# New order tables for the five engines of a hybrid encoder layer

## The chip, the cores and the metric

The kernel runs on one core of a Trainium2 chip. The metric is the device time of one execution in microseconds (us). The engines are called PE (TensorE), DVE (VectorE), ACT (ScalarE), POOL (GpSimd) and SP (SyncE, which here issues all the data transfers). "L1762" is line 1762 of the kernel.

## The reference

One layer of a streaming encoder is computed in fp32 for 1024 prompt frames and 64 frames of a running stream with 512 cached positions. Cut to what matters:

```python
D_MODEL, SEQ, DEC_SEQ, PAST_LEN, D_FF = 1024, 1024, 64, 512, 4096
H_FOX, H_SGU, H_SB = 6, 4, 6                       # heads of 64 columns each

q_f, k_f, v_f, log_f, u_g, v_g, q_s, k_s, v_s = in_proj(x, w_in, b_f)   # one projection
c = cumsum(log_f, axis=1)
# forgetting attention: causal softmax with logit + c_t - c_s
o_f = softmax(where(mask, q_f @ k_f.T / 8 + c_q - c_k, -1e30)) @ v_f
# spatial gating in chunks of 128 positions, w_s lower triangular
o_g = gelu(u_g) * (w_s @ layer_norm(gelu(v_g)) + b_s)
# stick-breaking attention, strictly causal
a = exp(log_sigmoid(z) + sum of log_sigmoid(-z) over the positions between)
o_s = where(mask, a, 0) @ v_s
mix = (rms_norm_per_head(concat(o_f, o_g, o_s)) * g_mix) @ w_out
x = layer_norm(ALPHA * x + mix, ln1_g, ln1_b)
x = layer_norm(ALPHA * x + square(relu(x @ w_up)) @ w_down, ln2_g, ln2_b)
```

The new keys, values and log gates of the attention are outputs too.

## The kernel before

Every fp32 operand of a matmul is split into a high part, a copy rounded by ACT, and a low part, the difference, which a helper at L120 (`lo_sub`) takes on DVE or POOL. A product is then three passes on PE: high by high, high by low, low by high. Weights come from memory as f32 (`raw`, `rwo`, `wr`, `rd`), are copied by ACT (L344, L987, L1238) and subtracted at L120 or L988.

The stages follow each other, with overlaps:

1. Input. Blocks of 128 rows of x (`xr`, loaded at L318) are transposed on PE (`xtp`, L327) into `xT`. The projections `kvfox`, `kvsb`, `sgu`, `sgv` run at L368, and the queries (`qfox`, `qsb`) at L509. The head queries are scaled into `qd` (L517, L518), whose other half is copied across partitions by a small transfer (L128).
2. Attention. For each head and pair of query blocks, scores `S` (L567), then for the forgetting heads a reduction with the gate on DVE (`m`, L539) and an exponential on ACT (`T`, L542); for the stick-breaking heads a scan on DVE (L551) and additions on POOL (L553). The rows are transposed on PE (`pt`, L615), split into `pth` (ACT at L583, DVE at L120) and multiplied by the values (`o`, L625 to L628). Meanwhile the rows of w_out are scaled by g_mix (`rwo` loaded at L980, `swo` at L987) and stored to memory (`wo_dr`, L991).
3. Output projection (`mx`, L257) and the first layer norm.
4. Up-projection by a fast scheme that adds and subtracts blocks of the operands first and needs fewer products: banks `zA` to `zD` (L1300) are combined on DVE into `hh` (L1314 to L1320), squared after a relu (L1332), and summed (L1341 to L1344). Sums and blocks are stored (`h_dr`).
5. Down-projection in the same scheme: banks `A`, `B`, `D` (L1762), `h4a` and `h4b` as split operands (L1464). Bank by bank the results are added into `acc` on DVE (L1727 the first time, with the residual, and L1729 later). `awa` holds one of the accumulators for a time. L1432 makes the sums of the weights.
6. Tail. The last additions give row sums as well (L1772), then follow the negated mean (L1836), the squares on ACT (L1841), the scale on POOL (L1831, L1832), and the normalisation, on ACT and POOL (L1856, L1860, L1864) for some blocks and on DVE (L1872, L1874) for others, and the stores (L1865, L1875).

Loops over heads, blocks and panels write the instructions, but they do not set the order that is run. At the end of the build `set_orders` takes the instructions of each engine's queue and chains them in the order of a table, one per engine, so that each queue runs exactly in that order. An instruction whose inputs or buffers are not ready holds all that stand behind it on its engine. Buffers and banks were assigned before that and are the same whatever the tables say. The tables are text: numbers packed and encoded, unpacked by `unpack`.

Of the kernel before, what the change touches and what calls it, by code (L numbers as in the profile page):

```python
# [78 lines left out]
def _build(nc, tc, a, es):  # L79
# [2046 lines left out]
{OJW)cPA8^wfrvs+zwO{7qDCS^%JuEb>zkOQLg91<KD=sH_e-cSiW8I<SZm}A7juu(Va3!Hn#A4L-_Y6<<&hPT4c-`+1T~f6z<&yN;2=XYFB`-!((uLz
99SkWuPzdCXZoxKIj!q(6kos_3)aX8m>KHY>u`Cck}Xa{{1FFnY;MsK~ViH35-1xmRi@-`Li#Q>#1NPQy05cet%2q%6&#EMyK#<GWPKR`v#V-V}sdFUc
SUwVJ-j9@!GG+S=_6ib}Z>3SS@?G1FzTet8whFvTiKLso(L^^=u-Jw1R(@8GihPX!xfby$jQ3&{$VW^xz7Ki;Vru;NbxCL`4Kao`%HM4Mwy{to=WL_EF
^MD3vLJ9wna764uq2U0K5WxXG#!Z}K^EEzoxj|J-N%kG%xX1<fKBW1K9B_R|TnGK({64L9-n%Pj7WH&?G&+VeW(;+wQHt@m58y^yPUva}JXcjm6^aQXc
rZ!?#SCj6A4QZ6;E!#hI4E|sM|@_(b#<8Ev>D1y>G*842xSD&_??;-MWke8<!?)JgjVV*}B_XVB@y-M?V=^5h1xU#U?u||ja^(|J5Kk}N{h(o{O<=b$E  # L2130
iH8vO8hts`bU#pR{v!V@g_-P!y!I=y<_A(w?;@V#lL2YC!?_;f>1{HD)!tiWr#G;Vk^Jd$)H$_^rSj9^J@Ftu@ujF2!PqYd2F-J3{xF%f80m&AdLFXT{
jq$n!KOB^RdK*WK8M<;ut9mVeTfY{4)z?jfadW)<7p1bGQU0eL|+G&1Qu2WM@iZ|gPvcVr!8?3Z_$#aO__z6J>Yua)t;8O89fv_)n)K)wS`}!<o_K66$
Fxu<&rMerOc5s@!sXAODm=C*TnU07cj@V&>4%kZxpjpXAkTLjZXT_g>SQpAniiL9^tKoBcGY6_G2j|UVQ_*Mq-)fTdjqB)12oDG5Yw7yr<FY4=^{fHo|
76d9%}vl@y%%sEIx7SzpgRymOFY`@zPvB4e$5<Vxa{4A%ZUfI!#cJ1>W8f;|;;%-%+jvdBbf!pgj1db}(rJlcvj>kK5Z#c*<e3%qPBUO8$|m(|0c4SJ2
U>YpT-^f3#qUceqFaQi1LLmm4_Fs62qX|X|{s+{q59nt9l#0xI*H1;&kDkEjE#*@&}6#NzXHBstVKW~1uRy*O3Omb|P(qTQ?DlaZ;LwP*~*|2&$f3_ol
Bl%HbBr2;3*s`LaHcugTZWES<2SyUIGnM#!bJ(vy#Zl|=sT0s7JzLvvVv&rN81+362;0Z1*OA!7EIw>PNi-x7<;zi2t1~5KcW>n_7kRB70%gA+B8Wz<Q
V;RSZi>uE+xYpU&dt(wB61~kb5I+Tx33J&Q~Mo7yvG><d#fVfeNs}p;VCoX-RwuEJQqJ&b3cygqCH-*##JVESx;hZ#=3#}Fv9y@ZcwN}@@{~~pI3N`tE
171vK0b_Cm{ySmLEO$8!dhQJ!tExdYYaEnbyFS(jOep9tRbP)sd(ygclU;mYbQEkzDi?{{51i-PNcmvr-W#nbi}J#0qCY<XLAMt0;Uq8dom^I|`i1E*v
S3ywyWQJ)2+S*f!eDK&@TG@2b4OZzX@4O*F<L+FT<MV6+pH4l!A?(<ZXm0L3Xd&}NWSN1Q6V)_`%8n^$kl(Hl&58k!_ZQ6H-@i-ZXt%tw7!NHK@pT?<#
poCVbYmllAIZd@GyP5|A?g1aUvVzhm!8=Toc4C?72(l=DQ8^Ws}K{Bc8i6VlbG>6HgZ`Ft~e;vk;XUw~6ejbA`7AuQ00#~mlV1=0_OVf={%mNv^e$Jis  # L2140
Fjk^fwH2#v@p>2}SMe0&Vr||Z-NQfMlfKO9oJKhc)zN!3GW#5t;Ay7sXCa#fE#d1`;p`IlF<5@yh{!`Hdr$RQau#Dr9*@%HrX=2CAn}qnfWG?(sQrt_W
G=DFSfraRF6%gTXmHLV<JfL&)>Pd4n?y3sq0HK1&}(tR_|$v6oDN0PBgP|q#K|V=H|;=sFe9k>F@!2KcB$TAT^*lyUvBdo4Zq8b&)GsUlqFUS+T@{srQ
!Evhw}{mzJ{Q0*WW{<=RoI){k_|f7%QETNWV3wyk7zP57?5_MLg@ysHd&<zfktkA-&X5$n6u5a7B3u6uHVA{vU%%%(9h{OttULlo6~QO0pkSS*%Hw+%e
PiGG+t|FlXsLwbIB<|0vJ4K$2;yAv+dDO!G(On+qe7b^zOUTe;m>d?#e*BuwT}RH@YR*Bq&*`5<*YKCoIkhkHz-_)*-isc;ajAu@+h4!J0>M$K8IE!Mx
<&wVd2N`~aALN+a(DvT8f&;R0+&`cHC7CH0CXFjhxS=md2t^NkS_u|**I}hIz(SAUem8t8@(w~lN$3@0Zo5xCg_R5rgCj{;thEP<$%;9Ed#Nx87y976;
$Xoj92_@fkSw~9FSacc<-wyw~TxN1^sc<poIb|YegcQ<hFQ6d@JuHf3yhC<`TAVcghVY}scn%^`yjHFy?K92m%XaQ08`1T)eFB@hBRp+Ru^ai;vkTPEw
<B|%V_m%zX*Hg-uauJgXryIqr@SqXciR!^yEWn~#VoY=>xkT40=f59kk_~uW*vL!;!ueH2O!;V`EXGt5}`9MC)-QC)Jwh8OTE-f9~70!-SrPLTi;6`6y
# [3 lines left out]
2x;Tyvyu}8uaH*yY!ltjsN))U9y9VM%~=kyf;2y0iSK;~l2i1829mSEbd@z9-8oiy`c6;DxaVAV=Fm%}r-`BS2vlCG9DNDfVzuX{clOkdUI$9EKj*rLJ
_?yx>#Zf_zW)rf=J#~qG$uXMq<>B6|JJwLoOZQ+Qh_6}UpWs9>W^JtWk#mI-@8QituUdLV`i(|{ns>=_#`X6ely1J+F)@u!I*udev&iCx}cA<EQRYemi
&x%G*_J7c?!b5oXg9>R;!&6jt{WrPfwV2M)*A%bv*g6s22b0^Glj{RK7I^u8Z{7V7R*0;<npojOQ%KWBbg~eusax4!`|fo0gyk9Ve}d$*<k$dE`L>{*?
q}dLwBuEGpmoBK7uc>HgYP=vS=qo~*`5QhPO(607KLV}F#9N^3roBDR9A>E$G1+39ezPw-6KcFR5u=htt8`fbQIu&s6mbvg}48B6E)rhs(#>qaG|-ooY
`kUe(sW0H4)o~W}U?Q(qPAf)GP{{Q)!W>14IWUeAV`Y*>4r|1
# [51 lines left out]
A5E=@EP@7tH*h|!n`FerKN4s-t7B~!u^olrrTtXVX8xP?G@vd?fQss7?*PNTQm$io_VWp%xepIGR~WU^YEXq8_$00y@1ugtBgkO4OjRl1E<5E^arYaib  # L2207
# [26 lines left out]
```

## Time and profile before

| | us |
|---|---|
| median of 3 runs (lowest to highest) | 1385.33 (1384.52 to 1386.87) |
| the profiled execution | 1386.09 |
| its span, first to last instruction | 1384.4 |
| PE busy | 1317.4 (95%), 8827 matmuls |
| DVE busy | 980.4 (71%) |
| ACT busy | 728.0 (53%) |
| POOL busy | 606.4 (44%) |
| mean granted clock of PE | 0.994 |

An engine counts as busy while it runs an instruction, not while it waits or issues a transfer. A row of the timeline gives start, busy time, engine, line, operation, output and inputs, shapes, and how many alike follow each other; in brackets stands how long the engine was idle before it and what it then waited for. Matmuls overlap in the pipeline, so one that shows 0.4 us can follow another after 0.2 us. Waits of an engine are listed as: who waited for whom, us in total, times, longest.

### The profile page before, as it was taken

The numbers are of one execution on the slowest core, as the hardware profiler recorded it, in microseconds if no ns is written. First come the engines' busy times: TensorE is split into PE (matmuls) and PEld (weight loads), VectorE is DVE, ScalarE is ACT, GpSimd is POOL, SyncE is SP. The second block draws the span as 40 slices with busy tenths as digits, with TensorE's granted clock in tenths as the row PEclk, the third lists the DMA queues.
The fourth block names the chain that finished last, engine by engine and source line by source line (L and its number), as shares of the span: only waits on it lengthen the run. The fifth ranks groups of instructions, "written<-read, shape, count | busy, mean of one in ns | idle before, by whom it ended". The sixth has DMA issues, their size and how long they took to land.

```text
span 1384.4 us, 24306 instructions
## 1 busy us (share of the span) xinstructions
PE 1317.4 (95%) x8827; PEld 1197.6 (87%) x8827; DVE 980.4 (71%) x1795; ACT 728.0 (53%) x1561; POOL 606.4 (44%) x667
## 2 busy tenths in 40 slices
PE   7888899999999999999999999999989999999996
PEld 7888899989998899777799999999977778887874
DVE  4566656566788368779865878777786777767776
ACT  4465646466666466334432323223266676767773
POOL 3221313226666354676512212212176675665556
PEclk9999999999999999999999999999999999999999
DMA  8655414132221346632234444444558344435333
GB/s 254 181 164 169 131 50 127 42 80 67 76 51 42 82 131 219 222 118 84 76 118 152 142 146 142 134 154 142 183 186 289 127 134 167 141 118 172 113 116 121
DMA packets 159088, 185.62 MB, mean 134 GB/s; under 512 B 27757, under 2 KB 117165, under 8 KB 158969
## 3 DMA queue, kind: packets, MB, share of 16 engines
q1 hardware_dynamic: 158968, 184.08, 42.0%
q8 instruction: 69, 1.13, 0.3%
q14 instruction: 51, 0.41, 0.1%
HBM read 117.65 MB, written 60.10 MB: 128 GB/s over the span
## 4 chain that ended last, share of the span: by engine, by line
PE 53%; DVE 11%; DMA 5%; ACT 4%; POOL 4%; issue 3%; SPq 0%; POOLq 0%; DVEq 0%; ACTq 0%
PE A L1762 9%; PE zA L1300 8%; PE mx L257 7%; PE zD L1300 5%; PE D L1762 5%; PE kvsb L368 3%; PE zB L1300 3%; PE zC L1300 3%; PE B L1762 2%; DMA h_dr<-hh 1%; PE sgv L368 1%; DVE snsb L551 1%; DMA raw<-w_in 1%; PE sgu L368 1%; PE ds L1808 1%
## 5 line engine op out<-in xcount | busy, mean ns | idle before, releaser
L120 POOL TENSOR_TENSOR wa<-wr,wa 128x512 fp32r<-128x512 f32 x42 | 60.2, 1462 | 231.9 <-ACT wa L1238 231.9
L120 POOL TENSOR_TENSOR wd<-rd,wd 128x512 fp32r<-128x512 f32 x77 | 105.1, 1379 | 105.8 <-ACT wd L1238 78.3
L257 PE MATMUL mx<-xT,oTb 128*128 128x512 f32 (+1 forms) x416 | 104.3, 401 | 0.7 <-ACT oTb L215 0.5
L1300 PE MATMUL zD<-xo,ws 128*128 128x288 f32 (+1 forms) x720 | 98.7, 290 | 2.1 <-DVE hh L1314 2.1
L1300 PE MATMUL zA<-xo,ws 128*128 128x288 f32 (+1 forms) x720 | 97.3, 289 | 0.0
L1300 PEld LDWEIGHTS zD<-xo,ws 128*128 128x128 f32 x720 | 93.7, 189 | 3.5 <-DVE hh L1314 3.4
L368 PE MATMUL kvfox<-wkvfox,xT 128*128 128x256 f32 (+3 forms) x624 | 92.2, 294 | 2.0 <-ACT wkvfox L344 1.0
L1300 PEld LDWEIGHTS zA<-xo,ws 128*128 128x128 f32 x720 | 93.6, 189 | 0.0
L1311 ACT ACTIVATE sn<-zA 128x256 f32<-128x256 f32 (+1 forms) x80 | 31.0, 391 | 117.7 <-PE zA L1300 103.0
L257 PEld LDWEIGHTS mx<-xT,oTb 128*128 128x128 f32 (+1 forms) x416 | 74.9, 186 | 19.3 <-DVE oTb L120 1.0
L368 PE MATMUL kvsb<-wkvsb,xT 128*128 128x256 f32 (+1 forms) x624 | 89.3, 287 | 1.0 <-ACT wkvsb L344 0.9
L1762 PE MATMUL A<-wd,wd 128*128 128x512 f32 x312 | 84.9, 398 | 3.3 <-DVE acc L1729 3.3
L553 POOL TENSOR_TENSOR sgsb<-sgsb,snsb 128x127 f32<-128x127 f32 (+7 forms) x48 | 59.1, 1235 | 64.4 <-DVE snsb L551 55.4
L368 PEld LDWEIGHTS kvfox<-wkvfox,xT 128*128 128x128 f32 (+1 forms) x624 | 82.5, 193 | 2.9 <-ACT wkvfox L344 1.4
L1432 POOL TENSOR_TENSOR rd<-rd 128x512 f32<-128x512 f32 x56 | 76.6, 1368 | 11.5 <-DVE b L120 8.9
L1238 ACT ACTIVATE wd<-rd 128x512 fp32r<-128x512 f32 x105 | 63.9, 623 | 32.8 <-POOL rd L1432 18.0
L368 PEld LDWEIGHTS kvsb<-wkvsb,xT 128*128 128x128 f32 (+1 forms) x624 | 79.4, 187 | 1.8 <-ACT wkvsb L344 1.1
L551 DVE TENSOR_TENSOR_SCAN snsb<-snsb,one 128x128 f32<-128x128 f32 (+7 forms) x48 | 68.0, 1422 | 13.9 <-ACT snsb L550 12.6
L1762 PEld LDWEIGHTS A<-wd,wd 128*128 128x128 f32 x312 | 59.0, 190 | 18.7 <-DVE acc L1729 4.6
L1729 DVE TENSOR_TENSOR acc<-acc,A 128x512 f32<-128x512 f32 x73 | 49.6, 682 | 30.7 <-PE A L1762 30.7
L1762 PE MATMUL A<-wd,h4a 128*128 128x512 f32 x240 | 64.7, 393 | 0.0
L120 DVE TENSOR_TENSOR pthfox<-ptfox,pthfox 128x512 fp32r<-128x512 f32 (+1 forms) x60 | 37.6, 635 | 31.9 <-ACT pthfox L583 31.5
(548 smaller groups left out, 3723.7 us busy)
## 6 DMA issues: line engine op xcount, KB each, us to landing
h_dr<-hh SPq DMA_DIRECT2D x30, 512.0 KB, 3.4
rd<-w_down SPq DMA_DIRECT2D x30, 512.0 KB, 4.3
wr<-w_up SPq DMA_DIRECT2D x13, 1024.0 KB, 5.5
hr<-h_dr SPq DMA_DIRECT2D x31, 384.0 KB, 3.4
h_dr<-hh SPq DMA_DIRECT2D x30, 384.0 KB, 3.9
raw<-w_in SPq DMA_DIRECT2D x44, 256.0 KB, 3.8
wo_dr<-swo SPq DMA_DIRECT2D x32, 256.0 KB, 3.0
xT<-wo_dr SPq DMA_DIRECT2D x8, 1024.0 KB, 7.3
```

What stands on the lines that cost most here:

```text
L120: eng.tensor_tensor(out, src, hi.bitcast(F32), op=ALU.subtract)
L257: nc.tensor.matmul(acc[0:m], oT[:, k, hx, 0:m], wo[k // 4][hw][:, k % 4, cs], start=(i == 0), stop=(i == len(seq) - 1))
L368: nc.tensor.matmul(acc[0:n, c0:c0 + n1 - n0], xT[k // 4][:, k % 4, c:c + n], wt[:, k, hw, n0:n1], start=(i == 0), stop=(i == len(seq) - 1))
L551: nc.vector.tensor_tensor_scan(g[:, 0:n][:, ::-1], g[:, 0:n][:, ::-1], one.broadcast_to([P, n]), 1.0, op0=ALU.mult, op1=ALU.bypass)
L553: nc.gpsimd.tensor_tensor(s[:, 0:n - 1], s[:, 0:n - 1], g[:, 1:n], op=ALU.mult)
L1238: nc.scalar.activation(hi, raw, AF.Copy)
L1300: nc.tensor.matmul(z, w[:, hw, k], xop(s, bo, hx)[:, k, :], start=(new and k == 0 and j == 0), stop=(k == 3 and j == 2), skip_group_check= ...
L1311: nc.scalar.activation(c, z, AF.Copy)
L1432: eng.tensor_tensor(r[:, o], r[:, x], r[:, y], op=ALU.subtract)
L1729: nc.vector.tensor_tensor(out, out if other is None else other, bank, op=ALU.add)
L1762: nc.tensor.matmul(z, h[:, hx, q, o], wset[self.c % 2][q][:, hw, wb], start=((n in (0, 3) or n == 1 and self.c == 0) and q == 0 and j == 0 ...
L1808: nc.tensor.matmul(z[0:TS], hs[:, q, f, 0], w[:, 1], start=False, stop=(q == 1 and f == 1), skip_group_check=True)
```

## The change

The five tables in `ORDERS` are replaced. They come from the same kind of search over orders, run again with other durations in its model: steps with values of one row, the time of DVE and POOL while they work side by side, and transfers are taken as traces showed them. Nothing else differs: every instruction, buffer, bank and transfer is the same.

```diff
 ORDERS = {
     "PE": r"""
-c-rk-d5oP^6~8lY_I;)^)0ycqr87e}N*4=VX`yzbST+MDRMZ$F8VtcTM1}Z|3eiMDf^|VEO0-ZK1QfA_A{4vXLR%><U8X9nU8mI2eermgbMJTV_PzJ8)
...
+c-oy@36zz^m9BpMUhf-p({wkzplnSuK(iT8P|zsgf`+(dj7dyP%t<omjAl6|ag2%P%*is7xFi$LWSry}lPDOY=D0;Ct_g#pB0-Q%x|N;orlG;^M!i#Y>
...
```

What it moves is shown at three places. In the rows stand the line, the operation, output and inputs with their numbers, and the shape; "x4" means four alike in a row.

The first place is the start. On SP, the loads before; `raw_0_138` and `raw_1_142` are the gate's six columns of w_in, the other `raw` pieces 128 columns:

```order
L318 DMA xr_117<-x_prompt 128x1024
L343 DMA raw_0_120<-w_in 128x4x128
L318 DMA xr_128<-x_prompt 128x1024
L343 DMA raw_0_130<-w_in 128x4x128
L343 DMA raw_1_134<-w_in 128x4x128
L343 DMA raw_0_138<-w_in 128x4x6
L343 DMA raw_1_142<-w_in 128x4x6
L318 DMA xr_146<-x_prompt 128x1024
L318 DMA xr_148<-x_prompt 128x1024
L343 DMA raw_1_124<-w_in 128x4x128
```

And after:

```order
L318 DMA xr_117<-x_prompt 128x1024
L343 DMA raw_0_138<-w_in 128x4x6
L343 DMA raw_1_142<-w_in 128x4x6
L343 DMA raw_0_120<-w_in 128x4x128
L343 DMA raw_1_124<-w_in 128x4x128
L318 DMA xr_128<-x_prompt 128x1024
L343 DMA raw_0_130<-w_in 128x4x128
L673 DMA cache_fox_k_0_930<-cache_fox_k 128x2x128
L673 DMA cache_fox_v_0_932<-cache_fox_v 128x2x128
L673 DMA cache_fox_k_1_934<-cache_fox_k 128x2x128
L343 DMA raw_1_134<-w_in 128x4x128
L318 DMA xr_146<-x_prompt 128x1024
```

The gate's columns come forward, the third block of x (`xr_146`) goes behind three loads of the cache. On PE at the same place, before:

```order
L327 MATMUL xtp_0_211<-ident,xr_128 128x128 x4
L327 MATMUL xtp_1_218<-ident,xr_128 128x128 x4
L368 MATMUL kvfox_0_177<-wkvfox_119,xT_109 128x262
L368 MATMUL kvfox_1_225<-wkvfox_119,xT_109 128x262
L327 MATMUL xtp_0_261<-ident,xr_146 128x128 x4
L327 MATMUL xtp_1_268<-ident,xr_146 128x128 x3
L368 MATMUL kvfox_0_177<-wkvfox_119,xT_109 128x262 x11
```

And after:

```order
L327 MATMUL xtp_1_218<-ident,xr_128 128x128 x2
L368 MATMUL kvfox_0_177<-wkvfox_119,xT_109 128x262
L327 MATMUL xtp_1_218<-ident,xr_128 128x128 x2
L327 MATMUL xtp_0_211<-ident,xr_128 128x128 x4
L368 MATMUL kvfox_0_177<-wkvfox_119,xT_109 128x262 x8
L368 MATMUL kvfox_1_225<-wkvfox_119,xT_109 128x262
L368 MATMUL kvfox_0_177<-wkvfox_119,xT_109 128x262 x2
```

The transposes of `xr_146` no longer stand between the first products of kvfox; the first of them comes after 27 of these.

The second place is the change from up- to down-projection, on DVE. `hh_0_12434` is the last panel's block, whose relu (L1332) and sums (L1341 to L1344) stand among the first additions from the banks into the accumulators. Before:

```order
L1332 SCALAR_TENSOR_TENSOR hh_0_12434<-hh_0_12434 128x1152
L1727 SCALAR_TENSOR_TENSOR awa<-awa,A_0_12596 128x512
L1727 SCALAR_TENSOR_TENSOR acc_12586<-acc_12586,A_1_12603 128x512
L1341 TENSOR_TENSOR hh_0_12434<-hh_0_12434 128x256
L1344 TENSOR_TENSOR hh_0_12434<-hh_0_12434 128x256
L1342 TENSOR_TENSOR hh_0_12434<-hh_0_12434 128x256
L1727 SCALAR_TENSOR_TENSOR acc_12587<-acc_12587,D_0_12672 128x512
L1727 SCALAR_TENSOR_TENSOR acc_12588<-acc_12588,D_1_12679 128x512
```

And after:

```order
L1341 TENSOR_TENSOR hh_0_12434<-hh_0_12434 128x256
L1464 TENSOR_TENSOR h4b<-hx,st_12668 128x512
L1729 TENSOR_TENSOR acc_12586<-acc_12586,B_1_12634 128x512
L1727 SCALAR_TENSOR_TENSOR acc_12587<-acc_12587,D_0_12672 128x512
L1727 SCALAR_TENSOR_TENSOR acc_12588<-acc_12588,D_1_12679 128x512
L1729 TENSOR_TENSOR acc_12587<-acc_12587,A_0_12596 128x512
L1729 TENSOR_TENSOR acc_12588<-acc_12588,A_1_12603 128x512
L1342 TENSOR_TENSOR hh_0_12434<-hh_0_12434 128x256
L1464 TENSOR_TENSOR h4b<-awa,st_12708 128x512
L1343 TENSOR_TENSOR hh_0_12434<-hh_0_12434 128x256
L1344 TENSOR_TENSOR hh_0_12434<-hh_0_12434 128x256
```

Three of the four sums now stand behind the additions that empty the D banks (the fourth, L1343, stood behind them before too, seven rows below the last one shown).

The third place is the tail, again on DVE. `acc_12590` and `acc_12746` are the accumulators that are finished last; `A_1_15490` and `lastD` are banks that end in the second of them. Before:

```order
L1872 SCALAR_TENSOR_TENSOR acc_12590<-acc_12590,ident,gbp_15465 128x512
L1872 SCALAR_TENSOR_TENSOR acc_12590<-acc_12590,ident,gbp_15467 128x512
L1729 TENSOR_TENSOR acc_12746<-acc_12746,A_1_15490 128x512
L1729 TENSOR_TENSOR acc_12746<-acc_12746,lastD 128x512
L1874 SCALAR_TENSOR_TENSOR acc_12590<-acc_12590,ident,gbp_15469 128x512 x2
```

Five rows further down, still before:

```order
L1836 TENSOR_SCALAR ident<-ident 128x1
L1872 SCALAR_TENSOR_TENSOR acc_12746<-acc_12746,ident,gbp_15465 128x512
L1872 SCALAR_TENSOR_TENSOR acc_12746<-acc_12746,ident,gbp_15467 128x512
L1772 ISA acc_12746,ident<-A_1_15490,acc_12746 128x512
L1772 ISA ident 128x1
L1836 TENSOR_SCALAR ident<-ident 128x1
```

And after, the same two stretches in one:

```order
L1729 TENSOR_TENSOR acc_12746<-acc_12746,A_1_15490 128x512
L1872 SCALAR_TENSOR_TENSOR acc_12590<-acc_12590,ident,gbp_15465 128x512
L1872 SCALAR_TENSOR_TENSOR acc_12590<-acc_12590,ident,gbp_15467 128x512
L1729 TENSOR_TENSOR acc_12746<-acc_12746,lastD 128x512
L1874 SCALAR_TENSOR_TENSOR acc_12590<-acc_12590,ident,gbp_15469 128x512
L1772 ISA acc_12746,ident<-A_1_15490,acc_12746 128x512
L1772 ISA ident 128x1
L1874 SCALAR_TENSOR_TENSOR acc_12590<-acc_12590,ident,gbp_15471 128x512
L1772 ISA acc_12746,ident<-lastD,acc_12746 128x512
L1772 ISA ident 128x1
L1836 TENSOR_SCALAR ident<-ident 128x1
L1772 ISA acc_12746,ident<-A_1_15490,acc_12746 128x512
```

The addition from `A_1_15490` moved ahead of the two L1872 rows, and the very last L1772, with the L1836 behind it, ahead of the first two L1872 rows of `acc_12746`.

More of the change, by code (lines that the diff above doesn't have):

```diff
@@ L2126 @@
[L2126 to L2135, printed above, removed]
@@ L2151 @@
[L2151 to L2155, printed above, removed]
+c-oy@36zz^m9BpMUhf-p({wkzplnSuK(iT8P|zsgf`+(dj7dyP%t<omjAl6|ag2%P%*is7xFi$LWSry}lPDOY=D0;Ct_g#pB0-Q%x|N;orlG;^M!i#Y>
@@ L2188 @@
[L2188 to L2191 removed]
+c-mc7%Wfl85H0u9?<7tp$z)(N5?ek1goMNo%mO6D0`U!qe_+iQAb|uD5)1YSi9LUS7^LAblT4CHY^UArw!1jz-0PVUmh5idN8M9Zr%qk7%*@tqR^VCtz
```

164 lines of the change are left out of this document (100 added, 64 removed).

## The prediction

> **What bounds the kernel now.** I read the page's engine totals first, then busy time by stretches of the span, then the waits of TensorE (PE), then the timeline at each long wait.
>
> ```profile
> PE 1317.4 (95%) x8827; PEld 1197.6 (87%) x8827; DVE 980.4 (71%) x1795; ACT 728.0 (53%) x1561; POOL 606.4 (44%) x667
> ```
>
> PE carries the time. The table below has, for each stretch, its length, then busy time and count of PE, weight loads, VectorE (DVE), ScalarE (ACT) and GpSimd (POOL), then the granted clock.
>
> ```profile
> 0.00:34.60 34.60, 26.30 (x182) 24.80 (x183) 16.86 (x32) 16.38 (x33) 10.42 (x30) 1.00 0.88 254
> 34.60:69.20 34.60, 30.30 (x236) 29.07 (x235) 20.70 (x51) 14.07 (x36) 8.98 (x16) 0.95 0.69 181
> 69.20:138.40 69.20, 61.11 (x470) 57.36 (x469) 44.46 (x121) 38.75 (x93) 12.24 (x27) 0.98 0.54 167
> 138.40:276.90 138.50, 131.98 (x1072) 127.28 (x1071) 81.36 (x231) 78.75 (x197) 34.87 (x68) 1.00 0.32 87
> 276.90:415.30 138.40, 132.06 (x1075) 127.74 (x1075) 100.68 (x196) 89.68 (x229) 76.44 (x104) 1.00 0.27 68
> 415.30:553.80 138.50, 130.43 (x1046) 124.22 (x1044) 93.80 (x170) 85.83 (x216) 71.63 (x92) 1.00 0.41 119
> 553.80:692.20 138.40, 133.05 (x695) 107.71 (x695) 113.64 (x197) 59.86 (x108) 93.20 (x89) 1.00 0.37 125
> 692.20:1003.70 311.50, 310.42 (x2459) 309.36 (x2458) 227.82 (x353) 89.20 (x163) 60.24 (x42) 1.00 0.43 146
> 1003.70:1038.30 34.60, 30.77 (x191) 27.59 (x191) 28.68 (x38) 20.96 (x43) 25.85 (x16) 0.98 0.56 186
> 1038.30:1315.20 276.90, 276.74 (x1192) 220.58 (x1191) 203.12 (x314) 194.24 (x382) 168.89 (x140) 1.00 0.47 158
> 1315.20:1349.80 34.60, 32.81 (x142) 25.58 (x141) 27.13 (x52) 27.53 (x52) 20.39 (x20) 1.00 0.33 115
> 1349.80:1384.40 34.60, 21.43 (x90) 16.36 (x88) 22.16 (x48) 12.75 (x20) 23.26 (x25) 0.91 0.32 121
> ```
>
> Read length minus PE busy. The up-projection (692 to 1004) has 1.1 us to give, the down-projection (1038 to 1315) 0.2: there another order can win nothing. The slack is 8.3 + 4.3 + 8.1 us up to 138, 6.5 + 6.3 + 8.1 us from 138 to 554, 5.4 us up to 692, 3.8 us around the change from up- to down-projection, 1.8 + 13.2 us at the end: 67 us in all. With the same 8827 matmuls, this is the most that an order can win, beyond the half-speed stretches counted below. Some of it is owed: the first matmul waits 4.25 us for the first transfer, and the last rows must be normalised and stored.
>
> **The sum.** It is made against the profiled execution, 1386.09 us, which stands 0.76 us above the median 1385.33. No instruction is added or taken away, so the only costs are waits.
>
> *Head, 0 to 17 us.*
>
> ```profile
> 7.73 1.97 PE L327 MATMUL xtp<-ident,xr 128*128 128x128 f32 x8 [1.55 <-DMA xr<-x_prompt]
> 10.68 0.80 PE L368 MATMUL kvfox<-wkvfox,xT 128*128 128x262 f32 x2 [0.98 <-ACT wkvfox L344]
> 12.65 1.73 PE L327 MATMUL xtp<-ident,xr 128*128 128x128 f32 x7 [1.16 <-DMA xr<-x_prompt]
> 14.03 3.16 PE L368 MATMUL kvfox<-wkvfox,xT 128*128 128x262 f32 x15
> ```
>
> Before, only two kvfox products run at 10.68, because PE's next rows are seven transposes of the third block of x, which land late (1.16 us). After, those transposes stand behind 27 kvfox products, and the two weight pieces of 24-byte rows are second and third on SP, not sixth and seventh. The block and the weights for the first product still amount to the same bytes, so its start near 10.7 stays. I take away the 1.16 us and a quarter of the 0.98: **-1.4**. Ends: +1 (the 24-byte pieces delay all behind them) and -3 (all but 0.7 of the three waits).
>
> *The wait at 60 us and the clock.*
>
> ```profile
> 56.09 1.09 PE L368 MATMUL kvfox<-wkvfox,xT 128*128 128x256 f32 x7 [0.75 <-POOL wkvfox L120]
> 60.23 0.41 PE L567 MATMUL Sfox<-kpfox,qdfox 128*128 128x128 f32 x2 [3.05 <-DMA qdfox<-qdfox]
> 60.48 3.40 PE L368 MATMUL kvfox<-wkvfox,xT 128*128 128x256 f32 x16
> 53.73 0.49 SPq L128 DMA_DIRECT2D qdfox<-qdfox  x1
> ```
>
> The first scores wait 3.05 us for a small copy issued at 53.73. The 16 products after it take 3.40 us, 0.21 each, where seven at 56.09 took 1.09, 0.156 with their pipeline end: PE runs at half speed (this stretch's clock is 0.95), which costs some 1.7 us more. After, two wo_dr stores, which SP issued before that copy, stand behind it and its twin, but the weight loads (raw) still stand ahead, and just one kvfox product, not eight, stands directly ahead of the scores on PE, 0.8 us less cover. I take 2 of the 4.75 us: **-2**; ends +2 (cover lost, stores no obstacle) and -4.75.
>
> [...]
>
> *Attention, 69 to 554 us.*
>
> ```profile
> PE ofox L625 <- ACT pthfox L583: 5.5, 5, 2.3
> PE Sfox L567 <- DVE mfox L539: 4.1, 6, 1.3
> ```
>
> These are the largest groups of the whole run (total, times, longest); the rest are smaller, so there are many waits of about 1 us and no single cause. The product o waits for ACT's copy pth, which waits for the transpose pt. I laid the two orders side by side, taking PE's rows between a producer and its user at their spacing, and each row on the other engines at its median with an assumed 0.12 for each hand-over: places whose cover is shorter than the bare chain go from 34, lacking 12.9 us, to 27, lacking 7.7. That is an estimate, without queues. Median distance from pt to o hardly moves (3.3 to 3.1 us). Against it speaks ACT's own queue:
>
> ```profile
> 113.36 0.72 ACT L987 ACTIVATE swo<-rwo,gmx 128x512 fp32r<-128x512 f32 x1 [3.13 <-DMA rwo<-w_out]
> 124.99 0.38 PE L625 MATMUL ofox<-pthfox,vpfox 128*128 128x256 f32 x1 [2.26 <-ACT pthfox L583]
> DMA rwo<-w_out: 14.2, 8
> rwo<-w_out SPq DMA_DIRECT2D x13, 256.0 KB, 3.8
> ```
>
> ACT stands before swo until rwo lands (eight times, 14.2 us), with the pth copies queued behind. In the new order four of these loads have only 1.2 to 3.2 us of PE work between issue and swo (3.7 to 10 before), less than the 3.8 us a load takes. I take 5.2 from the covers, and give 3.2 back: **-2**. Ends -10 (a third of the 29 us) and +10.
>
> *From mixer to MLP, 676 to 692 us.*
>
> ```profile
> 678.01 1.84 PE L1300 MATMUL zB<-xo,w 128*128 128x288 f32 x12 [1.00 <-DVE xr L1194]
> 690.03 0.38 PE L1300 MATMUL zA<-xo,w 128*128 128x256 f32 x1 [1.84 <-DVE xo L120]
> ```
>
> DVE's splits xo now stand ahead of L1314 and L1316 (0.44 us each), and more products lie between. **-1**, ends 0 and -2.84.
>
> *From up- to down-projection, 1019 to 1041 us.*
>
> ```profile
> 1021.49 1.89 PE L1300 MATMUL zD<-xo,ws 128*128 128x288 f32 x12 [1.03 <-DVE hh L1314]
> 1032.75 0.84 PE L1762 MATMUL D<-wd,h4a 128*128 128x512 f32 x3
> 1033.43 0.39 PE L1762 MATMUL A<-wd 128*128 128x512 f32 x1
> 1036.84 0.63 PE L1762 MATMUL D<-wd 128*128 128x512 f32 x1 [2.79 <-DVE acc L1727]
> 1037.27 0.63 PE L1762 MATMUL A<-wd,h4b 128*128 128x512 f32 x1
> 1033.27 1.50 DVE L1344 TENSOR_TENSOR hh<-hh 128x256 f32<-128x256 f32 x1
> 1034.70 1.49 DVE L1342 TENSOR_TENSOR hh<-hh 128x256 f32<-128x256 f32 x1
> 1036.11 1.27 DVE L1727 SCALAR_TENSOR_TENSOR acc<-acc,D 128x512 f32<-128x512 f32 x2
> ```
>
> The additions that free D stand behind two sums of 1.5 us on DVE, which runs without a pause there. After, the sums stand behind the additions: 2.99 us sooner, less one h4b row now ahead of them, some 0.64 like an addition. On PE 65 down products, not 50, lie ahead of the waiting one; three take 0.68 from 1032.75 to 1033.43, 0.23 each, so 15 are 3.45 us. Together 5.8 us of cover against a wait of 2.79: it goes, and with it the half speed after it (0.43 from the product at 1036.84 to the next; the stretch of half clock at 60 us lasted about 3.4 us, and half of it, 1.7, is lost). Late next are the stored sums (L1344), read much later. **-4.5**; ends -1 (only five products lie between D's last first-round product and its next, 1.15 us against 0.67 plus hand-overs) and -5.5.
>
> *Tail.*
>
> ```profile
> 1366.94 1.41 DVE L1872 SCALAR_TENSOR_TENSOR acc<-acc,ident,gbp 128x512 f32<-128x512 f32 x2 [0.77 <-ACT hx L1841]
> 1368.27 0.68 DVE L1729 TENSOR_TENSOR acc<-acc,A 128x512 f32<-128x512 f32 x1
> 1369.00 1.66 PE L1762 MATMUL A<-wd,wd 128*128 128x512 f32 x6 [2.24 <-DVE acc L1729]
> ```
>
> The addition that frees A stands behind two L1872 rows (1.41 us), which themselves wait 0.77 us for ACT. After, it stands ahead of both, so 2.1 us go from PE's wait. The last L1772 and L1836 also move ahead of the four normalising rows of the block before, so the last squares can start soon after PE ends; the end is then four rows of 0.75 us and four shorter ones, and a store. **-3**, ends -1 and -4.5.
>
> Sum: -1.4 - 2 - 2 - 1 - 4.5 - 3 = -13.9, so 1372.2; less the 0.76 between profile and median, 1371.4. I say 1371.
>
> **Rivals.**
> - *Only the junctions win.* Waits up to 554 us change places, none go. For it: 5.5 and 4.1 us there are spread over eleven waits, and the distances hardly change. Then -1 - 4.5 - 3 = 8.5 less: 1377.
> - *Much more is won.* All ends on the good side, -3 - 4.75 - 10 - 2.8 - 5.5 - 4.5 = -30: 1355; I put the case at about 1360. Against it: many covers are still shorter than a chain.
> - *Slower.* ACT's queue is held by rwo at those four places. One costs the wait of 113 us, 3.13, plus 1.7 of half clock, 4.8 us. Four make 19; with the head and 60 us unimproved and the junctions' 8.5 won, +11: 1396. With two, it breaks even near 1386, so from three on it decides. Against it: pth copies may stand ahead of swo.
> - *Nothing happens.* The tables hold other orders, but engines run ahead in either, and the gains in one stretch are paid in another: 1385.
>
> **How the numbers follow.** 0.2% (2.8 us) is about what can be told from no change. My forecast, 1365 to 1375, has 0.45; only the junctions 0.18; much more 0.13; slower 0.15; nothing 0.09. Faster gets the first three, 0.76; same 0.09; slower 0.15. The range reaches from 1356, which leaves out little of the large gain, to 1390, which leaves out the worse half of the slower case.
>
> **What would show it.** No wait over 1 us on D at the change to the down-projection, and clock 1.00 there; PE's last products starting about 2 us after the ones before them or less; the wait for qdfox below 1.5 us; PE busy share near 96%. Wrong would be: ACT idle over 14 us before swo and new long waits of ofox behind pth between 30 and 170 us, or new stretches of clock 0.5 in the attention.

## The result and the profile after

| | us |
|---|---|
| new kernel, median of 4 runs | 1366.82 (1366.26 to 1369.76) |
| old kernel, median of 4 runs | 1386.1 (1384.52 to 1387.16) |
| ratio, 95% interval | 0.9866 [0.9848, 0.9884] |
| span of the profiled execution | 1364.5, before 1384.4 |

The new order is 19.3 us faster. The prediction's sum is 13.9 us, which leads from the old median of 1385.33 to 1371.4, given as 1371. The totals of the page after, and busy time by the same stretches as in the prediction:

```profile
span 1364.5 us, 24263 instructions
PE 1320.1 (97%) x8827; PEld 1194.5 (88%) x8827; DVE 999.4 (73%) x1795; ACT 729.0 (53%) x1561; POOL 606.8 (44%) x667
```

```profile
34.60:69.20 34.60, 30.25 (x245) 28.93 (x243) 22.18 (x53) 14.46 (x37) 7.84 (x16) 1.00 0.75 185
69.20:138.40 69.20, 66.30 (x536) 63.59 (x535) 52.52 (x146) 47.12 (x117) 16.47 (x31) 1.00 0.66 190
138.40:276.90 138.50, 137.68 (x1132) 134.06 (x1131) 85.87 (x239) 82.34 (x202) 33.87 (x70) 1.00 0.31 85
...
692.20:1003.70 311.50, 308.85 (x2422) 306.05 (x2422) 224.04 (x334) 96.25 (x180) 70.28 (x47) 1.00 0.45 149
1003.70:1038.30 34.60, 34.60 (x165) 28.62 (x164) 30.39 (x45) 20.60 (x40) 30.52 (x24) 1.00 0.78 278
1038.30:1315.20 276.90, 274.72 (x1173) 214.26 (x1173) 208.09 (x311) 194.63 (x380) 170.09 (x136) 1.00 0.42 143
```

PE is short by 2.9 us from 69 to 138 (8.1 before) and by 0.8 from 138 to 277 (6.5 before), the change of projections is full, and the granted clock is 1.00 in all of these. (One stretch of half speed is left in the new kernel before the tail, 3.41 us from 531.11.) But the up-projection is now short by 2.7 us (1.1 before) and the down-projection by 2.2 (0.2 before). The longest waits of PE after:

```profile
PE xtp L327 <- DMA xr<-x_prompt: 6.8, 2, 4.3
PE ptsb L615 <- DVE pthsb L120: 3.1, 4, 1.1
PE Ssb L567 <- ACT snsb L550: 2.6, 4, 1.2
PE Sfox L567 <- DVE mfox L539: 2.2, 4, 0.9
PE Sfox L567 <- DVE cum L434: 1.8, 1, 1.8
```

The waits for the query copy and for D are gone. Apart from the blocks of x at the start, no single wait is longer than 1.9 us, and in this list the waits of the stick-breaking attention (`sb`) now stand ahead of those of the forgetting one (`fox`).

Stretches of the clock no longer hold the same work in both. So I made a ledger by work: each matmul counts as its median distance to the next (119 ns for 256 columns, 134 for 288, 231 for 512, 109 for a transpose), 1264 us in all, and at a given amount of work the starting times in two traces are compared. "Lead" is how much earlier the new kernel's PE got there.

| PE work done, us | what lies before it | start before, us | start after, us | lead, us |
|---|---|---|---|---|
| 40 | head | 54.1 | 53.6 | 0.5 |
| 80 | first gates and scores | 106.7 | 100.3 | 6.3 |
| 270 | forgetting attention | 325.2 | 303.8 | 21.4 |
| 600 | stick-breaking attention, output projection | 685.5 | 670.5 | 15.0 |
| 620 | from mixer to MLP | 708.4 | 690.8 | 17.6 |
| 880 | up-projection | 968.9 | 955.3 | 13.5 |
| 980 | change of projections | 1077.4 | 1058.2 | 19.2 |
| 1210 | down-projection | 1313.1 | 1298.6 | 14.5 |
| end | tail | 1384.4 | 1364.5 | 19.9 |

By the end of the forgetting attention the lead is larger than at the end. Behind it 13.7 us are won and 15.2 lost. Here are two stretches of the ledger as busy time, in the columns of the prediction's table: the forgetting attention before and after, then the stick-breaking attention with the output projection before and after.

```profile
106.70:325.20 218.50, 203.89 (x1630) 195.60 (x1630) 133.39 (x352) 128.12 (x314) 60.85 (x110) 0.99 0.36 99
100.30:303.80 203.50, 199.92 (x1629) 193.52 (x1629) 133.85 (x351) 126.20 (x311) 61.10 (x110) 1.00 0.40 111
```

```profile
325.20:685.50 360.30, 346.48 (x2429) 313.55 (x2429) 267.95 (x479) 199.68 (x463) 215.49 (x255) 1.00 0.36 109
303.80:670.50 366.70, 353.18 (x2429) 316.02 (x2428) 281.98 (x482) 201.72 (x464) 217.16 (x257) 1.00 0.35 107
```

In the forgetting attention PE idles 3.6 us instead of 14.6, and its products take 4.0 us less, of which some 1.7 is the stretch of half speed at 125.70, now gone (an estimate, half of its 3.40 us). About half of the waits that go are those of the product o for ACT's copy pth, 5.5 us before and 0.5 after. In the stick-breaking stretch PE's idle time hardly changes (13.8 and 13.5 us). What is lost there is 6.7 us of busy time: the products follow each other at longer distances. The half speed at 531 makes some 1.7 of it, by half of its 3.41 us; what makes the rest isn't shown.

### The profile page after: what moved, and what is told of

It reads as the page before. It is cut to its first block, busy times and chain, and to the rows that moved or that the text cites. A ratio compares the mean times of both kernels' runs of the same rounds, so it can differ in the third digit from the quotient of the medians.

```text
span 1364.5 us, 24263 instructions
## 1 busy us (share of the span) xinstructions
PE 1320.1 (97%) x8827; PEld 1194.5 (88%) x8827; DVE 999.4 (73%) x1795; ACT 729.0 (53%) x1561; POOL 606.8 (44%) x667
## 4 chain that ended last, share of the span: by engine, by line
PE 73%; DVE 11%; ACT 5%; DMA 5%; issue 3%; POOL 3%; SPq 0%; DVEq 0%; ACTq 0%; POOLq 0%
PE A L1762 10%; PE zA L1300 9%; PE mx L257 7%; PE zD L1300 7%; PE kvsb L368 5%; PE D L1762 4%; PE kvfox L368 4%; PE zC L1300 3%; PE zB L1300 3%; PE B L1762 2%; DVE snsb L551 2%; PE Sfox L567 1%; PE ptfox L615 1%; PE qfox L509 1%; PE qsb L509 1%
## 5 line engine op out<-in xcount | busy, mean ns | idle before, releaser
L1300 PE MATMUL zD<-xo,ws 128*128 128x288 f32 (+1 forms) x720 | 111.2, 290 | 1.6 <-DVE hh L1314 1.4
L1300 PE MATMUL zA<-xo,ws 128*128 128x288 f32 (+1 forms) x720 | 109.7, 291 | 0.6 <-ACT sn L1311 0.6
L1300 PEld LDWEIGHTS zD<-xo,ws 128*128 128x128 f32 x720 | 98.1, 189 | 2.8 <-DVE hh L1314 2.4
L1300 PEld LDWEIGHTS zA<-xo,ws 128*128 128x128 f32 x720 | 97.6, 188 | 1.8 <-ACT sn L1311 0.9
L1762 PE MATMUL A<-wd,wd 128*128 128x512 f32 x312 | 90.6, 395 | 0.8 <-DVE acc L1729 0.8
L553 POOL TENSOR_TENSOR sgsb<-sgsb,snsb 128x127 f32<-128x127 f32 (+7 forms) x48 | 59.7, 1245 | 69.2 <-DVE snsb L551 61.2
L1238 ACT ACTIVATE wd<-rd 128x512 fp32r<-128x512 f32 x105 | 64.1, 623 | 25.6 <-POOL rd L1432 17.6
L1762 PE MATMUL A<-wd,h4a 128*128 128x512 f32 x240 | 69.5, 394 | 0.0
L1300 PE MATMUL zC<-xo,wa 128*128 128x288 f32 (+1 forms) x360 | 59.0, 289 | 0.0
```

Source lines behind the costliest of these rows:

```text
L553: nc.gpsimd.tensor_tensor(s[:, 0:n - 1], s[:, 0:n - 1], g[:, 1:n], op=ALU.mult)
L1238: nc.scalar.activation(hi, raw, AF.Copy)
L1300: nc.tensor.matmul(z, w[:, hw, k], xop(s, bo, hx)[:, k, :], start=(new and k == 0 and j == 0), stop=(k == 3 and j == 2), skip_group_check= ...
L1762: nc.tensor.matmul(z, h[:, hx, q, o], wset[self.c % 2][q][:, hw, wb], start=((n in (0, 3) or n == 1 and self.c == 0) and q == 0 and j == 0 ...
```

## The experiments

In the first group, parts of the two orders are put together. "New up to 303.8 us" means every row that the new kernel's trace shows started by then, in the new order; what is left follows in the old order. Since such a set is complete in itself (whatever a row needs has started before it), each piece can be cut and joined in this way. The text gives cuts in us of PE work, as in the ledger.

**Does each stretch stand by itself?** Two kernels, cut at 270 us of PE work.

```diff
-all queues: old order
+fox_after: new order up to 270, the rest old
+fox_before: old order up to 270, the rest new
```

> The queues run in the new order up to 303.8 us of the new kernel (270 us of PE work, the forgetting attention), and what is left then follows in the old order. Theory that the stretches stand by themselves: the lead of 21.4 us that the new kernel has at that point is kept and nothing of the new order's later losses and gains comes: 1386 - 21.4 = 1364.7 us, within 2 us for the seam. Rival, that a lead is paid for later because the rest of the queues and buffers were laid out for another start: 1370 us or more, the lead shrinking visibly behind the seam.

> The reverse: the old order up to 325.2 us of the old kernel (270 us of PE work), then the new order. Stretches by themselves: no lead at the seam, then the new order's +5 us in the stick-breaking attention, -2.6 between mixer and MLP, +4 in the up-projection, -5.6 at the change of projections, +4.6 in the down-projection, -5.4 in the tail, in all about +1.5: 1387.5 us, within 2 us. Rival, that the new order's later stretches are worse only because they start from a lead: the losses shrink and the time is 1378 to 1383 us.

fox_after: 1365.98 us, ratio 0.985 [0.9835, 0.9866]. fox_before: 1387.92, ratio 1.0008 [0.9995, 1.0021]. Both came as if the stretches were independent. In fox_after the lead is 20.2 us at 280 and 20.4 at 1260; in fox_before the losses and gains come in the new kernel's places (7.2 us lost by 600, 4.6 at 640, 8.4 at 880, 3.3 at 980, 7.7 at 1200, 2.2 at the end). So the whole gain, as a sum, lies in the first 304 us, and the rest is a draw.

**Do three local moves do it?** These are the prediction's own mechanisms, one row or two at each place, in the old order.

```diff
 DVE, change of projections
-L1344 hh, L1342 hh, L1727 acc<-acc,D x2
+L1727 acc<-acc,D x2, L1344 hh, L1342 hh
 DVE, tail
-L1872 x2, L1729 acc_12746<-acc_12746,A_1_15490
+L1729 acc_12746<-acc_12746,A_1_15490, L1872 x2
 SP, 52 us
-L991 wo_dr, raw, L991 wo_dr, L128 qdfox, L415, L128 qdfox
+raw, L128 qdfox, L415, L128 qdfox, L991 wo_dr x2
```

> The old order with three local moves only: two sums of the last panel (L1344, L1342) put behind the two additions from D on VectorE; one addition from A put ahead of the two L1872 rows in the tail; two stores of scaled weights put behind the two query copies on SyncE at 52 us. Theory of the prediction: the wait of 2.79 us at the change of projections and its half speed of 1.7 us go (-4.5), the wait of 2.24 us before the last products shrinks to about 0.2 (-2), the wait of 3.05 us for the query copy shrinks by half with its half speed (-2 to -3): about -9 us, 1377. Rival, that each place has a second wait right behind the first (D's products are only five apart, the tail is set by POOL's and ACT's chain, the copy is late because of the weight loads): -2 to -3 us, 1383.

1385.83 us, ratio 0.999 [0.9978, 1.0002]: nothing. The waits of PE in this kernel:

```profile
PE Sfox L567 <- DVE mfox L539: 6.7, 5, 3.4
PE xtp L327 <- DMA xr<-x_prompt: 6.0, 2, 4.3
PE ofox L625 <- ACT pthfox L583: 5.1, 6, 2.0
PE A L1762 <- DVE acc L1729: 3.1, 3, 1.2
...
PE A L1762 <- ACT h4a L1459: 1.8, 1, 1.8
```

The waits for the query copy (3.05 us) and for D (2.79) are gone, but each had another behind it. The copy is issued at 53.61 us, 0.12 earlier than in the old kernel, and PE reads it 3.50 us later without a wait, where in the old kernel it landed only after 6.4, so the two stores ahead of it had held it. After the copy came the gate: a new wait of 3.4 us for the reduction `mfox` at 73 us, with clock 0.95 now in this stretch, where it was 0.98, and 1.00 in the one before, where it was 0.95. The loss of clock moved with the idle time:

```profile
34.60:69.20 34.60, 31.98 (x256) 30.31 (x255) 21.01 (x51) 14.13 (x37) 9.10 (x16) 1.00 0.68 182
69.20:138.40 69.20, 58.88 (x450) 55.54 (x448) 45.01 (x123) 38.88 (x95) 12.22 (x27) 0.95 0.56 173
```

At the change of projections, PE ran on past D and stopped twice some 50 products later:

```profile
1044.98 0.96 PE L1762 MATMUL B<-wd,h4a 128*128 128x512 f32 x3 [0.89 <-DVE acc L1727]
1047.76 1.10 PE L1762 MATMUL A<-wd,h4a 128*128 128x512 f32 x2 [1.82 <-ACT h4a L1459]
```

Behind both stands ACT. It waited 6.09 us for a load of w_down (5.61 in the old kernel) and then worked without a pause up to h4a, while DVE, ahead of the addition that frees B, stood 2.64 us for a row of ACT:

```profile
1042.17 0.63 ACT L1238 ACTIVATE wd<-rd 128x512 fp32r<-128x512 f32 x1 [6.09 <-DMA rd<-w_down]
```

The half speed came back here too: the two products at 1047.76 take 1.10 us, where two at 1038.43 take 0.62. In the tail, the product that waited 2.24 us starts at 1367.59 instead of 1369.00, but the next two groups then wait 0.50 and 0.26 us, and the last begins at 1371.68. The rows behind it start where they did, since two L1872 rows still wait for ACT's squares, and the last L1772 stands behind them:

```profile
1374.52 1.41 DVE L1872 SCALAR_TENSOR_TENSOR acc<-acc,ident,gbp 128x512 f32<-128x512 f32 x2 [1.37 <-ACT hx L1841]
1375.84 0.68 DVE L1772 CUSTOM_DVE_ANT_0 acc<-A,acc 128x512 f32<-128x512 f32 x1
```

**What is behind the query copy?** The gate's way is: sums on DVE (L438, L441, L445), stored to memory (`c_dr`, L450), read back for all partitions (`cbfox`, L1027), reduction (L539). In the old order L988, DVE's half of a scaled weight block, stands between L438 and L441, and needs ACT's half, which waits for a load. The next kernel has the SP move alone of the three and adds that row, and on SP the gate's store `c_dr` ahead of the stores behind L988.

```diff
 DVE
-L438 cum, L988 swo, L441 car, L574, L445 cum
+L438 cum, L441 car, L574, L445 cum, L988 swo
 SP, besides the move at 52 us
-L991 wo_dr, p_fox_k, p_fox_v, L991 wo_dr, L980 rwo, L450 c_dr
+L450 c_dr, L991 wo_dr, p_fox_k, p_fox_v, L991 wo_dr, L980 rwo
```

> The old order with moves at one place only, 52 to 66 us: the two stores behind the query copies on SyncE, as in the run of three moves, and in addition VectorE's half of a scaled weight block (L988, which waits for ScalarE and so for a load) put behind the rest of the gate's sums (L441, L445), with the gate's store (c_dr) ahead of the weight block's stores on SyncE. Theory: the gate's way through memory (sums, c_dr, cbfox, reduction L539) was the second wait right behind the query copy, and L988 held it; c_dr is issued near 63 us instead of 66, the 3.4 us wait for mfox near 73 us shrinks below 1 us, and PE is 3 to 5 us ahead by 90 us, which stays to the end: 1382. Rival, that a third chain (key tiles, row copies) ends at the same time: less than 1 us, 1386.

1383.74 us, ratio 0.9981 [0.9966, 0.9996]. In the ledger the lead is 2.9 us at 60 and 3.1 at 300, so the size is near the theory's lower end. DVE's timeline there:

```profile
60.98 0.16 DVE L441 TENSOR_TENSOR_SCAN car<-one,cum 6x7 f32<-6x7 f32 x1
61.06 0.28 DVE L574 TENSOR_TENSOR Sfox<-Sfox,m_fox 128x128 f32<-128x128 f32 x1
61.26 1.07 DVE L445 TENSOR_TENSOR cum<-cum,car 6x896 f32<-6x896 f32 x1
62.66 0.75 DVE L988 SCALAR_TENSOR_TENSOR swo<-rwo,gmx,swo 128x512 fp32r<-128x512 f32 x1 [0.33 <-ACT swo L987]
```

The new kernel has the same sequence:

```profile
61.15 0.17 DVE L441 TENSOR_TENSOR_SCAN car<-one,cum 6x7 f32<-6x7 f32 x1
61.34 0.30 DVE L574 TENSOR_TENSOR Sfox<-Sfox,m_fox 128x128 f32<-128x128 f32 x1
61.55 1.07 DVE L445 TENSOR_TENSOR cum<-cum,car 6x896 f32<-6x896 f32 x1
62.55 0.73 DVE L988 SCALAR_TENSOR_TENSOR swo<-rwo,gmx,swo 128x512 fp32r<-128x512 f32 x1
```

c_dr is issued at 62.36 here and 62.65 in the new kernel, 66.25 in the old one. In this run PE waits 1.55 us for mfox at 70.35, more than the 1 us expected; with the stores moved alone it was 3.4 us at 73. In the kernel of three moves the lead is 0.2 us at 60 and 1.2 at 120, so the move of the stores is worth little by itself. Which of the two rows added here counts, and what they do without that move, was not tried.

**Is it ACT that holds the attention, as the prediction's slower rival had it?** Eight of the swo rows that waited were moved three rows later, with their chains.

```diff
 ACT, for example at 113 us
-L987 swo, L638 osbfox, L469 kvsfox, L583 pthfox, L583 pthfox
+L638 osbfox, L469 kvsfox, L583 pthfox, L987 swo, L583 pthfox
 DVE L988, SP L991 x2 and the next L980: as much later
```

> The old order, in which eight of ScalarE's scalings of the output weights that waited for their load (swo, between 38 and 121 us) are moved three ScalarE rows later, with the rest of each chain (VectorE's half, the two stores, the next load) moved by as much time. Theory: ScalarE's standing before swo held the copies of the attention rows back; its idle time before swo falls from 14.2 us to under 6 and PE wins 3 to 5 us before 170 us: about 1382. Rival: other rows were late anyway (the gate's reductions on VectorE), ScalarE only waits elsewhere: within 1 us of 1386.

1401.27 us, ratio 1.0097 [1.008, 1.0114], 15 us slower: both theories failed. ACT's idle time before swo fell only from 14.2 to 13.0 us (five waits). The rows of this chain share one buffer each (L979, L984), so a later swo lets the next load start later, and the edit moved that load too. DVE's idle time before L988 rose from 15.3 to 17.6 us. The two largest groups of PE's waits between 30 and 170 us:

```profile
PE Sfox L567 <- DVE mfox L539: 9.3, 3, 4.6
PE ftp L432 <- DVE lf L404: 3.4, 1, 3.4
```

But waits are only half of the loss. From 20 to 120 us of PE work, old kernel first, then this one:

```profile
33.20:156.10 122.90, 109.21 (x844) 103.48 (x843) 78.51 (x209) 66.50 (x164) 27.33 (x48) 0.97 0.60 175
32.80:173.60 140.80, 118.50 (x844) 113.91 (x843) 78.81 (x209) 66.53 (x165) 26.62 (x48) 0.87 0.52 152
```

PE idles 8.6 us longer, and the same 844 products take 9.3 us longer, at a granted clock of 0.87 instead of 0.97. The mean clock of its four runs, 0.982 to 0.986, lies below that of the old kernel's runs beside it, 0.988 to 0.994.

In the new kernel this chain waits far less, on ACT (L987) and on DVE (L988); first before, then after:

```profile
ACT swo L987 <- DMA rwo<-w_out: 14.2, 8, 3.2
DVE swo L988 <- ACT swo L987: 15.3, 7, 3.8
```

```profile
ACT swo L987 <- DMA rwo<-w_out: 2.9, 3, 1.9
DVE swo L988 <- ACT swo L987: 5.6, 7, 1.9
```

So the chain of scaled weights can cost 15 us when it is placed badly. That its better place gives the new kernel its 15 us from 80 to 270 us of work isn't shown.

**Is the smooth change of projections paid for earlier?** Only the piece from 930 to 980 us of work in the new order.

```diff
-all queues: old order
+old up to 930, new up to 980, the rest old
```

> The old order with only the piece from 930 to 980 us of PE work in the new order (the change from up- to down-projection, 1020 to 1077 us of the old kernel). Theory that the smooth change is a matter of the order there: the 5.6 us that the new kernel wins in that piece come alone, 1381. Rival, that it is paid for earlier, in the up-projection, where the new order lost 4.1 us and VectorE's work for the change was done ahead: with that work still waiting at the seam, VectorE's queue is as long as before, and 0 to 1.5 us are won, 1385 or more.

1382.13 us, ratio 0.9971 [0.9955, 0.9987]. In the ledger 4.2 us are won between 940 and 980 and kept up to the tail. No wait for D is left, and the one of 1.03 us for hh is 0.33:

```profile
1019.79 1.89 PE L1300 MATMUL zD<-xo,ws 128*128 128x288 f32 x12 [0.33 <-DVE hh L1314]
```

So it is not paid for in the up-projection. This piece has the new order of all engines over some 50 us; the two rows of the prediction did nothing alone, and which other rows are needed isn't shown.

**Can the losses be left out?** Six kernels join the better piece of each stretch.

```diff
-all queues: new order
+sb_before: new to 270, old to 600, new
+two:       new to 270, old to 600, new to 640, old to 880, new
+three:     new to 270, old to 600, new to 640, old to 880, new to 980, old to 1200, new
+four:      new to 270, old to 510, new to 980, old to 1200, new
+five:      new to 270, old to 510, new to 640, old to 800, new to 980, old to 1200, new
+six:       new to 270, old to 510, new to 980, old to 1225, new
```

> The new order up to 270 us of PE work (303.8 us), then the old order up to 600 us of PE work (the stick-breaking attention and the output projection), then the new order. Stretches by themselves: lead of 21.2 at 600, 2.6 more between mixer and MLP, then the new order's +4.1, -5.6, +4.6, -5.4: 25.5 below before, 1361 us, some 6 us below the new kernel. Rival, that the new order's loss in the stick-breaking attention buys its gain behind it: 1365 to 1367.

> As the run before (old order from 270 to 600 us of PE work), and also the old order from 640 to 880 us of PE work (the up-projection), the new one for the rest. Stretches by themselves: 4 us less than that run, lead 23.8 at 880, 5.6 more at the change of projections, then +4.6 and -5.4: 30 below before, 1356 us. Rival, that the new order pays in the up-projection for its smooth change of projections (work of VectorE done ahead of time): the gain of 5.6 there does not come or halves, 1359 to 1362.

> As the run before, and also the old order from 980 to 1200 us of PE work (the down-projection), the new one for the tail. Stretches by themselves: 4.6 us less again, 35 below before, 1351.5 us. Rival, that a seam in the down-projection costs as much as it wins, since transfers and splits are prepared a panel ahead in another sequence: 1356 or more.

> New order up to 270 us of PE work, old from 270 to 510 (stick-breaking attention), new from there through output projection, up-projection and the change of projections up to 980, old from 980 to 1200 (down-projection), new for the tail. Stretches by themselves: lead 21.2 at 510, then 1.6 lost and 2.6 won up to 620, 1.6 won up to 980, nothing lost up to 1200, 5 won in the tail with 1 lost at the seam: 28 to 29 below before, 1357 to 1358 us. Rival, that every seam costs about 2 us: 1362.

> As the run before, with the old order also from 640 to 800 us of PE work (most of the up-projection). Stretches by themselves: 3.6 us that the new order lost there are saved, 1354. Rival, that the smooth change of projections is paid for in the up-projection: the seam at 800 gives the 3.6 us back before 980, 1357 to 1358.

> As the run named four, with the seam to the tail at 1225 instead of 1200 us of PE work. Stretches by themselves: the tail's gain comes all behind 1240, so nothing is lost, and 0 to 1 us is won if the seam at 1200 cost its 1.2 us by its place: 1356.5 to 1358. Rival, that the tail needs the additions and sums done ahead between 1200 and 1225: 1 to 3 us slower, 1359 or more.

| kernel | median, us | ratio to the old kernel, 95% |
|---|---|---|
| sb_before | 1362.54 | 0.9821 [0.9802, 0.9839] |
| two | 1364.85 | 0.9828 [0.9803, 0.9853] |
| three | 1359.81 | 0.9805 [0.9783, 0.9826] |
| four | 1358.85 | 0.9801 [0.9776, 0.9826] |
| five | 1356.09 | 0.9781 [0.9754, 0.9807] |
| six | 1360.65 | 0.9816 [0.9792, 0.9841] |

sb_before and four came within 2 us of their theories, and five within 2.1, but nearer to its rival (1357 to 1358). two and three missed theirs by 9 and 8 us; two also starts late (its lead is 16.5 us at 300, where sb_before has 20.4). six came as its rival had it. In sb_before the lead stays at 22.4 us from 480 to 600, where the new kernel falls to 15.0: the old order of the stick-breaking attention is better by itself. In three the lead is 23.8 at 980 and still 23.8 at 1200: so is the old down-projection. In the up-projection it isn't so clear: in two and three the lead is flat from 680 to 880 (19.6 and 21.1), but at the seam 3.5 and 2.0 us go by 900, in part in one new wait of 2.3 us for hh, near 960 us of the span. A seam at 800 (five) costs less by 840 (20.2 to 19.0) and the kernel is the fastest, yet the intervals of four and five overlap. The seam at 1225 (six) loses 2.8 us by 1240, the one at 1200 (four) 1.3. Five is faster than both kernels of the case (its interval ends at 0.9807, that of the new kernel begins at 0.9848; each was measured against the old one, not against the other):

```profile
span 1357.6 us, 24300 instructions
PE 1312.4 (97%) x8827; PEld 1194.5 (88%) x8827; DVE 982.8 (72%) x1795; ACT 728.3 (54%) x1561; POOL 602.9 (44%) x667
```

## Why the prediction was right, and where its steps were wrong

The sign, the size within 5 us and the range held. That the size came so near is in part luck: by the ledger the terms miss 22 us of gains and 15 us of losses, and these cancel in large part. The terms of the sum against the ledger, in us:

| term | forecast | ledger | what the runs showed |
|---|---|---|---|
| head | -1.4 | -0.5 | right in kind, within what repeats |
| 60 us | -2 | -5.8 | the gate behind it, not the copy alone |
| attention | -2 | -15.1 and +6.4 | two terms of opposite sign, both missed |
| mixer to MLP | -1 | -2.6 | right in kind |
| up-projection | 0 | +4.1 | no term was set up |
| change of projections | -4.5 | -5.7 | right size, wrong mechanism |
| down-projection | 0 | +4.7 | no term was set up |
| tail | -3 | -5.4 | right in kind, too small |

- *Attention.* The step that failed is the weighing of covers against the ACT chain, "5.2 from the covers, and give 3.2 back". The loads that it feared did not stand in the way: ACT's idle time before swo fell to 2.9 us, and the waits of o for pth to 0.5. The covers hid that the forgetting part gains and the stick-breaking part loses. The gain repeats: 13 to 16 us between 80 and 270 us of work in the new kernel and in the seven kernels joined with its start. What those counts left out, as the prediction says itself, is queues: they took each row at its bare duration, while a row can be late because of what stands ahead of it on its engine, as L988 ahead of the gate's sums. They also assumed 0.12 us for each hand-over; in the old trace an engine that had waited for another's row started 0.03 to 0.08 us after that row's end, by the median of each pair. And the two groups of waits shown are the largest only behind that of the head, 7.0 us for the blocks of x.
- *60 us.* The step took 2 of 4.75 us, on one move on SP. That move took the whole wait for the copy away, but alone it gave 0.2 us by 60; with L988 and `c_dr` moved as well it gave 3. Of the rest of the 5.8 no run shows the rows.
- *Change of projections.* The forecast of 4.5 was near 5.7, but not by the mechanism forecast. The step that failed is "Late next are the stored sums (L1344), read much later". With the two sums behind the additions the wait for D did go, but late next were B and h4a, behind ACT and its wait for a load of w_down, and PE lost 0.89 and 1.82 us there and the half speed again.
- *Up- and down-projection.* "There another order can win nothing" was right and half the story. Where PE is full, another order can still lose, 4.1 and 4.7 us here; 1.3 and 1.5 of these are new waits, the rest longer distances between products. The rival "gains in one stretch are paid in another" was right as a sum and wrong as a cause: the pieces can be parted.
- *Tail.* PE's earlier last products were worth nothing by themselves (1385.83 us with that move). In the new order PE's last product ends 3.8 us sooner, counted from 1210 us of work, and what follows takes 9.4 instead of 10.9 us. The second move named in the prediction, the last L1772 ahead of the normalising rows, fits the second part: ACT's two squares now follow each other at once around PE's end, where 2.39 us lay between them before. That move was not tried alone, so its share isn't shown. ACT's rows, before and then after:

```profile
1376.78 1.15 ACT L1841 ACTIVATE hx<-acc,ident 128x1024 f32<-128x1024 f32 x1 [2.39 <-DVE ident L1836]
```

```profile
1354.90 1.15 ACT L1841 ACTIVATE hx<-acc,ident 128x1024 f32<-128x1024 f32 x1 [5.41 <-DVE ident L1836]
1356.21 1.15 ACT L1841 ACTIVATE hx<-acc,ident 128x1024 f32<-128x1024 f32 x1
```

Of the signs that the prediction named, the wait for D is gone, the clock is 1.00 there, PE's last products follow each other without a wait, and PE is busy for 97%. One sign of being wrong came as well, a new stretch of half speed in the attention, at 531; it lies in the stretch that lost.

What stays open: which rows make the forgetting attention 15 us faster between 80 and 270 us of work, and which make the products of the stick-breaking one, and of the two projections behind it, follow each other more slowly.

## What to carry to other kernels

A wait's length, with the half speed behind it, is only the most that removing it can win (in `moves` the waits of 3.05 and 2.79 us went, and the time was 1385.83 against 1386.48 us): ask what the next row on the path waits for, and remove both, or expect little. With the instructions unchanged, compare two orders by work done, not by time; that shows stretch by stretch which is better, and pieces cut at a moment of a trace can be joined (here some 10 us better than the searched order), at a cost at some seams, 1 to 3.5 us here. A stretch without slack needs a term too: it can't win, but it can lose.

## What the runs showed of the hardware

- In the old kernel PE's half speed came after idle times of 3.05, 2.26 and 2.79 us, for 3.41 us each time, and not after the 2.24 us at 1369.00 (the six products there start 0.25 apart). With the wait at 60 us removed (`moves`), the clock from 34.6 to 69.2 us rose from 0.95 to 1.00, and the next stretch, with the wait of 3.4 us at 73, fell from 0.98 to 0.95. The length of one wait does not settle it: in the new kernel half speed came at 531, for 3.41 us, behind two waits of 0.77 and 1.08 us, and not after the wait of 1.82 us at 56.71 (clock 1.00 from 34.6 to 69.2). Three stretches of the old kernel by time, with the clock third from the end, then one of the new kernel and one of five:

```profile
60.84:64.26 3.42, 3.42 (x18) 3.42 (x17) 3.15 (x4) 1.02 (x2) 0.00 (x0) 0.50 1.07 270
125.70:129.10 3.40, 3.40 (x19) 3.40 (x18) 2.42 (x8) 2.36 (x5) 0.00 (x0) 0.50 0.19 43
1037.06:1040.47 3.41, 3.41 (x9) 2.64 (x9) 0.92 (x2) 0.60 (x1) 3.33 (x5) 0.50 0.93 265
```

```profile
531.11:534.52 3.41, 3.41 (x18) 3.37 (x17) 1.90 (x4) 2.12 (x5) 3.15 (x5) 0.50 0.84 271
478.66:482.07 3.41, 3.41 (x17) 3.41 (x16) 2.81 (x6) 2.96 (x8) 3.27 (x3) 0.50 0.43 127
```

- The same rows don't take the same time in every execution. Seven of these kernels run the same order up to 304 us; at 40 us of work their PE was at 53.3 (sb_before) to 55.6 us (two), at 120 us of work at 145.8 (four) to 149.9 (two). The four executions of two alone took 1359.09 to 1365.64 us. A difference of 3 us at the start in a single profile shows nothing here.
